# Weight sections of a two-layer encoder, fetched in one transfer or in two

## The chip, the cores and the metric

The kernel runs on one core of a Trainium2 chip. The metric is the device time of one execution in microseconds; lower is better. Before the change it is 2028.26 us, the median of three runs (2027.85 to 2029.19).

## What is computed

A two-layer encoder over 2048 tokens of width 1024. Each layer normalizes its input, projects it to eight parts of 512 columns, runs chunked softmax attention with a relative bias on one half of the heads and chunkwise retention on the other, gates both and projects back. Cut to what matters:

```python
def hybrid_layer(x, norm_gain, w_in, w_out, rel_bias, cos, sin):
    hn = rms_norm(x, norm_gain)
    proj = hn @ w_in                                   # (2048, 1024) @ (1024, 4096)
    aq, ak, av, ag, rq, rk, rv, rg = jnp.split(proj, cuts, axis=-1)
    ya = chunked_rel_attention(aq, ak, av, rel_bias)   # 8 heads x 64, own chunk and 8 before
    yr = chunkwise_retention(rq, rk, rv, cos, sin)     # 4 heads x 128
    y = jnp.concatenate([ya * silu(ag), yr * silu(rg)], axis=-1)
    return x + y @ w_out

def reference(x, positions, norm_gain, w_in, w_out, rel_bias, final_gain):
    for layer in range(2):
        x = hybrid_layer(x, ...)
    return rms_norm(x, final_gain)
```

All inputs are float32. w_in is (2, 1024, 4096), w_out is (2, 1024, 1024).

## The kernel before

Each float32 operand is split into a high and a low float16 part, and each product is taken as three float16 matmuls (high x high, high x low, low x high). A layer has four head groups (`s` = 0 to 3), each with two attention heads and one retention head, and each group goes over four blocks of 512 tokens (`n`). For a block, `dense_T` (L867) makes the transposed projections q, k and the two rotated parts, `dense_V` (L888) the projections with tokens on the partitions, and `attention` is interleaved with the dense matmuls of the next block: scores at L936 and L937, softmax on VectorE and ScalarE (L940 to L945), the low part of the probabilities `pq` on GpSimd (L946), a transpose of them by DMA into `pT` (L948), and the matmuls with v at L956 to L958. After the four groups the output projection `dO` (L1286) follows.

A group needs eight weight sections, each 1024 rows x 128 columns of w_in (512 KB): four for `dense_T` (tiles `stT`, by `prep_T`) and four for `dense_V` (`stV`, by `prep_V`). The output projection needs eight sections of w_out per layer (`stO`, by `prep_O`), and `prep_Omax` reads the same eight once more ahead of that for the scale (`stO0m`, `stO1m`). `load_sec` fetches one section into a tile of 128 partitions x 8 x 128 float32, where the row `k * 128 + p` lies on partition `p`, so each partition gets eight runs of 512 bytes. The tile is then squared and summed on ScalarE (L394), scaled and rounded to the high part on ScalarE (L419), and its low part is taken on VectorE (L422). The tiles come from a pool of three buffers (`w4`), shared with other staging tiles.

At the change of layers the sections for the next layer's first group are fetched by the other branch of `load_sec` (`halves`, L385), which has two smaller tiles and a transfer of 256 KB for each. The very first group of layer 0 is loaded with an order written by hand (`LOADS`): three of its sections by `load_sec` (names that begin with `T0_0`), the rest by transfers of their own.

All transfers are issued from SyncE, in one queue. On the compute engines the order is that of the program text, which tables such as `BESIDE` and `PLAN` set: a preparation is a generator, and each of its steps runs at a given half round of the dense matmuls. SyncE's order after the first block is left to the framework's scheduler. The program gives its transfers eight completion semaphores in turn. Among the transfers between which the loads stand are `swp` (halves of a rotated part swapped, L802 and L803), q and k copies (L771, L782 to L785), tables (`tabc`, `tabs`), outputs of a block (`y_d`, L971 and L1063) and the transposes of the normalized rows (`hTh`, `hTl`, L312 and L313).

Of the kernel before, what the change touches and what calls it, by code (L numbers as in the profile page):

```python
# [93 lines left out]
def hybrid_trunk(ctx: ExitStack, tc: tile.TileContext, x, pos, gain, gcol, w_in, w_out, rel, fgain,  # L94
# [4 lines left out]
    KT = D // P  # L99
# [4 lines left out]
    act, dve, pool, pe, sp = nc.scalar, nc.vector, nc.gpsimd, nc.tensor, nc.sync  # L104
# [269 lines left out]
    def load_sec(src, nm, halves=False):  # L374

        v = src.rearrange("(k p) c -> p k c", p=P)
        if not halves:
            st = w4.tile([P, KT, P], F32, tag="w4", name=f"st{nm}")
            sp.dma_start(st, v)
            return [(st, 0, KT)]  # L380
        h = KT // 2
        st = [b2.tile([P, 3 - i, 512], F16, tag=("rot2", "rot3")[i], name=f"st{nm}_{i}") for i in range(2)]
        st = [t_[:, 0:2].rearrange("p a c -> p (a c)").bitcast(F32).rearrange("p (k c) -> p k c", c=P) for t_ in st]
        for i in range(2):
            sp.dma_start(st[i], v[:, i * h:(i + 1) * h, :])  # L385
        return [(st[i], i * h, (i + 1) * h) for i in range(2)]
# [53 lines left out]
    class Sections:  # L440
# [12 lines left out]
        def load(self, j):  # L453
            o = TSEC[j] * 512 + self.s * P
            self.sts.append(load_sec(w_in[self.l, :, o:o + P], f"{self.nm}{j}", self.halves))
# [47 lines left out]
    def prep_V(l, s, g):  # L503
# [6 lines left out]
        def ld(j):  # L510
            o = VSEC[j] * 512 + c0
            sts.append(load_sec(w_in[l, :, o:o + P], f"{nm}{j}"))
# [39 lines left out]
    def prep_V_next(l, g):  # L552

        nm = f"V{l}_0"
        src = [w_in[l, :, VSEC[j] * 512:VSEC[j] * 512 + P] for j in range(4)]
        sts = [load_sec(src[j], f"{nm}{j}", True) for j in range(2)]
        yield
        for j in (2, 3):
            st = b2.tile([P, KT, P], F32, tag="q", name=f"st{nm}{j}")
            sp.dma_start(st, src[j].rearrange("(k p) c -> p k c", p=P))  # L560
            sts.append([(st, 0, KT)])
        yield
        g.vh = b3.tile([P, KT, 512], F16, tag="wh", name=f"wh{nm}")
        g.vl = b3.tile([P, KT, 512], F16, tag="wl", name=f"wl{nm}")
        hi, lo = ([w_[:, :, j * P:(j + 1) * P] for j in range(4)] for w_ in (g.vh, g.vl))
        m = [lowp_of(sumsq(sts[j], f"{nm}{j}", hi[j]), f"{nm}{j}") for j in range(2)]
        yield
        m2, m3 = (sumsq(sts[j], f"{nm}{j}", hi[j]) for j in (2, 3))
        m.append(lowp_of(m2 + m3, f"{nm}2"))
        yield  # L570
        yield
        iv = [None] * 3
        for j in (2, 0, 1):
            sv, iv[j] = norm_scale(allsum(m[j], f"{nm}{j}"), f"{nm}{j}", gains[l].i)
            for i in ((2, 3) if j == 2 else (j,)):
                yield from convert(sts[i], hi[i], lo[i], sv)
        yield from V_units(l, 0, g, iv, nm)
        g.vdone = 4
# [963 lines left out]
    for t in range(8, 16):  # L1542
        rows = late[t - 8] if t < 12 else xs0[t % 2]
        v = rows.bitcast(F16)
# [5 lines left out]
    for l in range(DEPTH):  # L1550
        gO = [Grp(), Grp()]
        go = Grp()
        for s in range(NSW):
            g = grp(l, s)
            for n in range(NS):
                first = (l, s, n) == (0, 0, 0)
                if not first:
                    st = states.setdefault((l, s, n), St())
                    dT = dense_T(l, s, n, g, st)
                else:  # L1560
                    st = st0
# [129 lines left out]
```

## Time and profile before

| what | value |
|---|---|
| median of three runs | 2028.26 us |
| profiled execution, its own time | 2024.23 us |
| its span (first to last instruction) | 2022.5 us |
| TensorE busy | 1986.4 us, 98% |
| VectorE, ScalarE, GpSimd busy | 1298.3, 1156.4, 464.0 us |
| granted TensorE clock, mean | 0.998 |
| bytes moved by DMA | 315.23 MB, mean 156 GB/s |
| transfers of the dynamic queue | 67.5% of the time of 16 DMA engines |

Times in the profile are microseconds from the span's start unless marked ns. PE is TensorE's matmul, PEld its weight load, DVE VectorE, ACT ScalarE, POOL GpSimd, SP SyncE; a q behind an engine's name means its sequencer, so SPq rows are issues of transfers, with the time that an issue kept the queue. A row of the timeline has start, duration, engine, line, operation, tiles and, in brackets, the idle time before it with what ended it. A row of the waits has the waiting engine and line, what it waited for, total us, number of times and the longest. A row of windows has the stretch, its length, then for TensorE, its weight loads, VectorE, ScalarE and GpSimd the busy time and the number of instructions, then the granted clock, the DMA engines' busy share and GB/s. A row of a line's instructions has minimum, median and maximum ns; "DMA to landing" is the time from issue to completion.

### The profile page before, as it was taken

The page shows a single profiled execution, that of the slowest core. Times are in us where ns is not written, and L with a number is a line of the kernel's source. Part 1 is how long each engine was busy: PE and PEld are TensorE (multiplying, and loading weights), DVE is VectorE, ACT ScalarE, POOL GpSimd, SP SyncE. Part 2 cuts the span into 40 slices and gives each one's busy share as a digit, 9 for nine tenths or more (in the row PEclk, how much of TensorE's full clock was granted, in tenths as well). Part 3 has the DMA queues.
Part 4 walks back from the last instruction along what each step waited for, and adds up shares of the span by engine and source line. Part 5 has one row for each costly group of instructions (what it writes and reads, how often), then busy time and mean ns, then how long its engine had stood idle before and what let it go on. Part 6 is the DMA issues. An engine that isn't in the chain of part 4 may idle for free.

```text
span 2022.5 us, 39569 instructions
## 1 busy us (share of the span) xinstructions
PE 1986.4 (98%) x14006; PEld 1047.4 (52%) x14006; DVE 1298.3 (64%) x4014; ACT 1156.4 (57%) x2525; POOL 464.0 (23%) x521
## 2 busy tenths in 40 slices
PE   6999999999999999999999999999999999999998
PEld 5444555555555555554444555555555555555444
DVE  7777867566656665766645557665666676557543
ACT  7666766466666655655445556655665665456432
POOL 1442222222222222220001222222222222222100
PEclk9999999999999999999999999999999999999999
DMA  9698765465586655899973547554755766558874
GB/s 265 137 185 189 156 147 132 103 140 129 131 182 139 155 128 104 191 243 269 241 180 95 123 99 161 122 119 100 158 123 133 168 162 160 120 119 191 207 205 125
DMA packets 654104, 315.23 MB, mean 156 GB/s; under 512 B 467505, under 2 KB 610865, under 8 KB 653905
## 3 DMA queue, kind: packets, MB, share of 16 engines
q1 hardware_dynamic: 653904, 312.70, 67.5%
q8 instruction: 110, 1.80, 0.4%
q14 instruction: 90, 0.73, 0.1%
HBM read 123.26 MB, written 41.98 MB: 82 GB/s over the span
## 4 chain that ended last, share of the span: by engine, by line
PE 88%; DVE 4%; DMA 3%; ACT 2%; SPq 1%; issue 1%; POOL 0%; ACTq 0%; POOLq 0%; DVEq 0%
PE dT L867 31%; PE dV L888 29%; PE dO L1286 13%; PE r L996 4%; PE S L937 3%; PE S L936 3%; PE o L956 2%; PE o L957 2%; PE o L958 2%; DMA pT<-pq 1%; PE dT L848 1%; DVE sc L940 1%; DMA swp<-raw 1%; ACT sc L943 0%; SPq L948 0%
## 5 line engine op out<-in xcount | busy, mean ns | idle before, releaser
L946 POOL TENSOR_TENSOR pq<-sc,pq 128x640 f16<-128x640 f32 (+4 forms) x256 | 328.7, 1284 | 1169.2 <-issue 717.0
L943 ACT ACTIVATE sc<-sc,mq,cT 128x640 f32<-128x640 f32 (+4 forms) x256 | 218.4, 853 | 426.3 <-DVE mq L942 423.6
L888 PE MATMUL dV<-whV,hTh 128*128 128x512 f16 x1024 | 352.3, 380 | 0.9 <-DVE gt L906 0.9
L888 PE MATMUL dV<-wlV,hTh 128*128 128x512 f16 x1024 | 352.3, 380 | 0.0
L888 PE MATMUL dV<-whV,hTl 128*128 128x512 f16 x1024 | 352.0, 379 | 0.0
L867 PE MATMUL dT<-hTh,whT 128*128 128x512 f16 x1008 | 346.6, 379 | 0.8 <-DMA hTh<-hTl 0.8
L867 PE MATMUL dT<-hTl,whT 128*128 128x512 f16 x1008 | 346.6, 379 | 0.0
L867 PE MATMUL dT<-hTh,wlT 128*128 128x512 f16 x1008 | 346.6, 379 | 0.0
L940 DVE CUSTOM_DVE_ANT_0 sc<-S,bias 128x640 f32<-128x640 f32 (+4 forms) x256 | 188.6, 737 | 192.8 <-PE S L937 191.6
L888 PEld LDWEIGHTS <-hTh 128*128 128x128 f16 x2048 | 196.6, 98 | 209.8 <-DVE gt L906 1.9
L867 PEld LDWEIGHTS <-whT 128*128 128x128 f16 x2016 | 192.3, 98 | 199.1 <-DVE gt L906 1.3
L945 ACT ACTIVATE pq<-sc 128x640 f16<-128x640 f32 (+4 forms) x256 | 171.5, 670 | 8.1
L1286 PE MATMUL dO<-whO,yly 128*128 128x512 f16 (+2 forms) x456 | 170.7, 375 | 1.6 <-DMA yly<-rly 1.6
L1286 PE MATMUL dO<-whO,yhy 128*128 128x512 f16 (+2 forms) x456 | 170.8, 375 | 0.3 <-DMA yhy<-rhy 0.3
L1286 PE MATMUL dO<-wlO,yhy 128*128 128x512 f16 (+2 forms) x456 | 170.8, 375 | 0.0
L888 PEld LDWEIGHTS <-hTl 128*128 128x128 f16 x1024 | 99.4, 98 | 104.3 <-issue 0.8
L867 PEld LDWEIGHTS <-wlT 128*128 128x128 f16 x1008 | 97.2, 98 | 100.7
L936 PE MATMUL S<-k,q 128*128 128x128 f16 (+3 forms) x592 | 142.4, 267 | 0.4 <-DVE mq L940 0.4
L1286 PEld LDWEIGHTS <-yhy 128*128 128x128 f16 x912 | 88.4, 98 | 101.6 <-DMA yhy<-rhy 0.8
L956 PE MATMUL o<-v,pT 128*128 128x65 f16 x1120 | 129.4, 193 | 9.7 <-DVE rl L962 4.6
L937 PE MATMUL S<-k,q 128*128 128x128 f16 (+3 forms) x592 | 129.7, 267 | 0.0
L957 PE MATMUL o<-v,pT 128*128 128x64 f16 x1120 | 129.7, 195 | 0.0
(374 smaller groups left out, 3388.8 us busy)
## 6 DMA issues: line engine op xcount, KB each, us to landing
q<-qq SPq DMA_DIRECT2D x128, 128.0 KB, 2.4
yyy<-y_d SPq DMA_DIRECT2D x32, 512.0 KB, 4.7
stT<-in_w_in_dram SPq DMA_DIRECT2D x27, 512.0 KB, 4.9
stV<-in_w_in_dram SPq DMA_DIRECT2D x26, 512.0 KB, 4.5
k<-kk SPq DMA_DIRECT2D x128, 64.0 KB, 2.1
tabc<-tab SPq DMA_DIRECT2D x32, 256.0 KB, 2.8
tabs<-tab SPq DMA_DIRECT2D x32, 256.0 KB, 2.7
y_d<-yr SPq DMA_DIRECT2D x128, 64.0 KB, 2.0
```

Of the source, the lines that this page charges most:

```text
L867: pe.matmul(ps, w_[:, j, kt, :], h_[:, kt, :], start=(m == 0), stop=(m == 23))
L888: pe.matmul(ps, h_[:, kt, a * P:(a + 1) * P], w_[:, kt, :], start=(m == 0), stop=(m == 23))
L936: pe.matmul(o, st.q[:, hx, 0, cs], k_, start=True, stop=False)
L937: pe.matmul(o, st.q[:, hx, 1, cs], k_, start=False, stop=True)
L940: dve.tensor_tensor_reduce(out=v, in0=S[:, 0:w], in1=g.bias[hx][:, 640 - w:640], scale=1.0, scalar=-3.0e38, op0=ALU.add, op1=ALU.max, accu ...
L943: act.activation(v, v, AF.Exp, bias=m[:, 0:1], scale=g.c[:, 0:1])
L945: act.activation(pq[:, 0:w], v, AF.Copy)
L946: pool.tensor_tensor(pq[:, w:2 * w], v, pq[:, 0:w], op=ALU.subtract)
L956: pe.matmul(o[:, 0:65], u.p[:, b, :], v_[:, 0:65], start=(b == 0), stop=False)
L957: pe.matmul(o[:, 0:64], u.p[:, b, :], v_[:, 65:129], start=False, stop=False)
L996: pe.matmul(out_, w_, m_, start=(i == 0), stop=(i + 1 == len(pairs)))
L1286: pe.matmul(ps, h_[:, kt, :], w_[:, kt, c0:c1], start=(m == 0), stop=(m == 23))
```

## The change

A section whose name begins with `T0_0` is fetched as before. For every other section that `load_sec` fetches into one tile, the transfer is cut into two: the first four of the eight runs of every partition, and then the last four.

```diff
         v = src.rearrange("(k p) c -> p k c", p=P)
         if not halves:
             st = w4.tile([P, KT, P], F32, tag="w4", name=f"st{nm}")
-            sp.dma_start(st, v)
+            n_ = 1 if nm.startswith("T0_0") else 2
+            for i in range(n_):
+                ks = slice(i * KT // n_, (i + 1) * KT // n_)
+                sp.dma_start(st[:, ks, :], v[:, ks, :])
             return [(st, 0, KT)]
```

80 sections are cut (24 of `stT`, 24 of `stV`, 16 of `stO` and 16 of `stO0m` and `stO1m`), so SyncE has 1479 transfers in place of 1399. The rows of the four compute engines stand as before. All lines below the change move down by three: the load is L382 then, the transpose of pT L951.

SyncE's queue at the first section that is cut, in layer 0, where group 1's first section `stT_10` is fetched during group 0. Before:

```order
L312 DMA_TRANSPOSE hTh_3_152<-xa 128x8x128
L379 DMA stT_10_2389<-in_w_in_dram 128x8x128
L802 DMA swp_0_2_3_2086<-raw_0_2_2014 64x512
L803 DMA swp_0_2_3_2086<-raw_0_2_2014 64x512
L313 DMA_TRANSPOSE hTl_3_153<-xa 128x8x128
L948 DMA_TRANSPOSE pT_0_1_2_0_2082<-pq_0_1_2_0_2079 128x10x128
```

The same place after:

```order
L312 DMA_TRANSPOSE hTh_3_152<-xa 128x8x128
L382 DMA stT_10_2389<-in_w_in_dram 128x4x128 x2
L805 DMA swp_0_2_3_2086<-raw_0_2_2014 64x512
L806 DMA swp_0_2_3_2086<-raw_0_2_2014 64x512
L313 DMA_TRANSPOSE hTl_3_153<-xa 128x8x128
L951 DMA_TRANSPOSE pT_0_1_2_0_2082<-pq_0_1_2_0_2079 128x10x128
```

One row has become two in the same place; what stands behind is the same.

A little later, `stT_13`, the fourth section of that group, between a pT and the four copies of k. Before:

```order
L379 DMA stT_13_2732<-in_w_in_dram 128x8x128
L948 DMA_TRANSPOSE pT_0_2_0_1_2576<-pq_0_2_0_1_2573 128x10x128
L782 DMA k_0_3_2608<-kk_0_3_2609 64x512
L783 DMA k_0_3_2608<-kk_0_3_2609 64x512
L784 DMA k_0_3_2608<-kk_0_3_2609 64x512
L785 DMA k_0_3_2608<-kk_0_3_2609 64x512
L948 DMA_TRANSPOSE pT_0_2_1_0_2680<-pq_0_2_1_0_2677 128x10x128
```

After:

```order
L382 DMA stT_13_2735<-in_w_in_dram 128x4x128
L951 DMA_TRANSPOSE pT_0_2_0_1_2578<-pq_0_2_0_1_2575 128x10x128
L785 DMA k_0_3_2611<-kk_0_3_2612 64x512
L786 DMA k_0_3_2611<-kk_0_3_2612 64x512
L787 DMA k_0_3_2611<-kk_0_3_2612 64x512
L788 DMA k_0_3_2611<-kk_0_3_2612 64x512
L382 DMA stT_13_2735<-in_w_in_dram 128x4x128
L951 DMA_TRANSPOSE pT_0_2_1_0_2683<-pq_0_2_1_0_2680 128x10x128
```

Here the scheduler puts a transpose and four copies between the two halves. This is so at 12 of the 80 sections, at some of them with only a `y_d` between.

The scan of w_out in layer 0, group 2, where three sections of `stO0m` are issued in a row. Before:

```order
L948 DMA_TRANSPOSE pT_2_1_2_0_8061<-pq_2_1_2_0_8058 128x10x128
L379 DMA stO0m_8117<-in_w_out_dram 128x8x128
L379 DMA stO0m_8186<-in_w_out_dram 128x8x128
L379 DMA stO0m_8225<-in_w_out_dram 128x8x128
L1063 DMA y_d_110<-yr_2_5_8163 128x128
```

After:

```order
L951 DMA_TRANSPOSE pT_2_1_2_0_8083<-pq_2_1_2_0_8080 128x10x128
L382 DMA stO0m_8141<-in_w_out_dram 128x4x128 x2
L382 DMA stO0m_8211<-in_w_out_dram 128x4x128 x2
L382 DMA stO0m_8251<-in_w_out_dram 128x4x128 x2
L1066 DMA y_d_110<-yr_2_5_8188 128x128
```

Six issues stand where there were three.

## The prediction

> **What bounds the kernel now.** I read the page first (engine shares, the chain that ended last), then the windows by stage, then the waits of TensorE and of SyncE's transfer queue, then the issue rows of the weight loads, and last the timeline around the loads that have something urgent behind them.
>
> ```profile
> PE 1986.4 (98%) x14006; PEld 1047.4 (52%) x14006; DVE 1298.3 (64%) x4014; ACT 1156.4 (57%) x2525; POOL 464.0 (23%) x521
> PE 88%; DVE 4%; DMA 3%; ACT 2%; SPq 1%; issue 1%; POOL 0%; ACTq 0%; POOLq 0%; DVEq 0%
> ...
> 200.00:850.00 650.00, 649.96 (x4867) 349.24 (x4866) 425.83 (x1407) 391.03 (x893) 160.07 (x178) 1.00 0.63 139
> 1000.00:1850.00 850.00, 849.91 (x6112) 449.32 (x6110) 529.49 (x1700) 485.82 (x1109) 190.65 (x217) 1.00 0.61 137
> ```
>
> TensorE is busy for 1986.4 of 2022.5 us. In the two long windows (first numbers after the length: TensorE) it is idle 0.04 us of 650 and 0.09 us of 850, at a granted clock of 1.00. Most of the changed loads lie there, and nothing that makes a load faster can be worth anything there. A change can cost, if it makes something late that TensorE takes just in time. What that would be is in the waits:
>
> ```profile
> PEld L956 <- DMA pT<-pq: 14.1, 13, 5.1
> PE o L956 <- DMA pT<-pq: 3.7, 3, 1.8
> ...
> SPq L948 <- POOL rss L1057: 218.2, 74, 5.8
> SPq L948 <- POOL pq L946: 194.7, 129, 10.6
> ...
> SPq L379 <- DMA x_d<-xxy: 4.6, 1, 4.6
> ```
>
> TensorE waits for the transposed probabilities pT. They leave by the transpose at L948, on the same queue as the weight loads of L379. The queue itself mostly waits in front of L948 for GpSimd, in 129 + 74 = 203 of 256 cases: there it is ahead of its work, and a longer issue somewhat earlier is swallowed. Only loads that run without a pause into an L948 count.
>
> **The change part by part.** The bytes, the pieces of 512 bytes (128 columns of 4) and all engine instructions stay; 80 loads become 160 transfers. What each half costs the queue is read from the loads of 512 KB (L379) and from the layer change, which already fetches halves (L385):
>
> ```profile
> L379 SPq DMA_DIRECT2D stT<-in_w_in_dram x27: 378/539/1675, 4.5 to 1497.4; - x27
> L379 SPq DMA_DIRECT2D stO1m<-in_w_out_dram x8: 383/552/1737, 1505.9 to 1572.1; - x8
> DMA to landing us min/median/max: 3.9/4.9/8.5
> ...
> L385 SPq DMA_DIRECT2D stT<-in_w_in_dram x8: 379/428/1219, 838.7 to 953.6; - x8
> DMA to landing us min/median/max: 3.1/4.2/5.3
> ```
>
> A whole load takes 0.539 us to issue, a half 0.428, with some 0.07 us to the next: 2 x 0.428 + 0.07 - 0.539 = 0.39, so I take 0.4 us more per load. [...] Over 80 loads that is 32 us of queue time; it counts at these places alone.
>
> First place: the first changed load, layer 0, second group.
>
> ```profile
> 157.51 0.57 SPq L379 DMA_DIRECT2D stT<-in_w_in_dram  x1
> 158.18 0.59 SPq L802 DMA_DIRECT2D swp<-raw  x1
> 158.82 0.59 SPq L803 DMA_DIRECT2D swp<-raw  x1
> 159.50 1.48 SPq L313 DMA_TRANSPOSE hTl<-xa  x1
> 161.08 4.75 SPq L948 DMA_TRANSPOSE pT<-pq  x1
> ...
> 162.92 0.38 PE L888 MATMUL dV<-whV,hTl 128*128 128x512 f16 x1
> 167.88 0.23 PE L956 MATMUL o<-v,pT 128*128 128x65 f16 x1 [4.58 <-DVE rl L962]
> ...
> 163.00:168.00 5.00, 0.42 (x5) 0.12 (x4) 2.26 (x8) 2.13 (x4) 0.57 (x1) 0.82 0.64 113
> 168.00:173.00 5.00, 5.00 (x29) 2.62 (x29) 4.96 (x13) 2.56 (x8) 1.83 (x1) 0.50 1.08 292
> ```
>
> The queue runs from 157.51 to 165.83 without a pause, and TensorE stands for 4.58 us behind it (and then runs at clock 0.50 for 5 us). Here 0.4 us more in front goes straight to TensorE: +0.4.
>
> Second place: two loads in front of a pT.
>
> ```profile
> 260.06 1.31 SPq L379 DMA_DIRECT2D stT<-in_w_in_dram  x2
> 261.60 1.53 SPq L1063 DMA_DIRECT2D y_d<-yr  x1
> 263.17 0.43 SPq L971 DMA_DIRECT2D y_d<-ya  x1
> 264.65 1.33 SPq L948 DMA_TRANSPOSE pT<-pq  x1
> ```
>
> The queue pauses from 263.60 to 264.65, 1.05 us; 2 x 0.4 = 0.8 is swallowed: 0.
>
> Third place: three loads of the scan for w_out's maximum.
>
> ```profile
> 575.29 2.94 SPq L379 DMA_DIRECT2D stO0m<-in_w_out_dram  x3
> 578.84 1.16 SPq L1063 DMA_DIRECT2D y_d<-yr  x1
> ...
> 581.05 0.38 SPq L714 DMA_DIRECT2D tabs<-tab  x1
> 581.89 1.58 SPq L948 DMA_TRANSPOSE pT<-pq  x1
> ```
>
> The pauses are 578.23 to 578.84 and 581.43 to 581.89, 0.61 + 0.46 = 1.07 us; 3 x 0.4 = 1.2, so 0.13 us is left. I count it whole, as if TensorE had no reserve. The same group in layer 1 I count as covered.
>
> Fourth place: a load of w_out directly ahead of a pT.
>
> ```profile
> 1807.22 0.57 SPq L379 DMA_DIRECT2D stO<-in_w_out_dram  x1
> 1807.91 3.47 SPq L948 DMA_TRANSPOSE pT<-pq  x1
> ...
> 1812.01 1.89 PE L888 MATMUL dV<-whV,hTh 128*128 128x512 f16 x8
> 1813.93 0.20 PE L956 MATMUL o<-v,pT 128*128 128x65 f16 x1
> ```
>
> TensorE ended its eight matmuls at 1813.90 and took pT at 1813.93, so there is no reserve: +0.4.
>
> Sum: 0.4 + 0 + 0.13 + 0.4 = 0.93 us. The profiled execution took 2024.23 us (span 2022.5), which would become 2025.2; the median of the three timed runs is 4.0 us above it, and the forecast goes from that: 2028.26 + 0.93 = **2029.2 us**.
>
> Two smaller edits. In 12 of the 80 pairs the scheduler puts other transfers between the halves (at stT_13 a pT and the four k copies), so these go out behind half a load, not a whole one. TensorE is idle 0.04 us of 650 there, so the gain is at most that: 0. And the program hands out eight completion semaphores in turn, so a transfer waits for the eighth before it to land, and a load now takes two of the eight. The longest such wait in the rows above is 4.6 us, once, on a store; with landings of 4.2 us and eight issues of 0.4 us or more ahead I count 0, up to a microsecond where loads stand together.
>
> [...]
>
> **The rivals.** *Slower, the queue has no room after all.* Three whole loads took 2.94 us, 0.98 each, where they stand together, and single issues reach 1.7. Let a half add p instead of 0.4. The places then cost p at the first and the fourth, 2p - 1.05 at the second, 3p - 1.07 at the third: 7p - 2.12 in all. From p = 0.88 this passes 4.06 us; at p = 1.2 (my estimate between 0.98 and 1.7) it is 6.3 us, **2034.6**; at 1.7 it is 9.8, 2038. For it: the issue rows just named. Against: the median of L385.
>
> *Slower, the weights land late.* If halves do not overlap, a load lands 2 x 4.2 - 4.9 = 3.5 us later.
>
> ```profile
> DMA to landing us min/median/max: 4.8/5.9/6.3
> ...
> 580.24 1.04 ACT L394 ACTIVATE stO0m<-stO0m 128x1024 f32<-128x1024 f32 x1
> ```
>
> The row is that of the three loads issued from 575.29: the first landed at 580.09 and ScalarE read it at 580.24. 3.5 us more would hold ScalarE for 3.35 us, and the probabilities behind it; once in each layer that is up to 6.7 us, **2035.0**. Against: all three landed within 6.3 us of issue, so loads do overlap, and elsewhere they come well ahead of use.
>
> *Faster, the standstill at 163 us gives way.* If with shorter transfers the swp copies and pT come 4.6 us sooner, TensorE keeps its clock too, and half of the 5 us at clock 0.50 is won: 4.6 + 2.5 = 7.1 us, **2021.2**.
>
> ```profile
> 895.00:905.00 10.00, 8.17 (x73) 4.36 (x72) 8.21 (x22) 6.43 (x12) 3.56 (x5) 1.00 1.04 243
> ```
>
> For it: an idle stretch of 1.8 us there left the clock at 1.00, so a shorter standstill would not bring it down. [...] Against: both halves of that load still stand directly in front of the copies.
>
> That the change does not do what it says is out but for the 12 pairs.
>
> **How the numbers follow.** The bound of 0.2%, about what a measurement of this kernel can tell from no change, is 4.06 us. Little change: 0.45. Slower by the queue: 0.30; by late weights: 0.08. Faster by the standstill: 0.17. So faster 0.17, same 0.45, slower 0.38. The likeliest case alone reaches from 2026 (the first and fourth places swallow it, and a microsecond of luck) to 2032. The whole range, 2022 to 2037, takes in the slower cases up to p = 1.55 and the lesser half of the faster one.
>
> **What would show it.** The new line (L382) should show 3 whole loads and 160 halves, these near 0.43 us each; SyncE's waits for GpSimd and VectorE should shrink by some 30 us in all; TensorE's two long windows should stay within 1 us of full. The forecast is wrong if the pT waits grow past 20 us, if ScalarE waits for stO0m or stT, or if the standstill at 163 us is gone.

## The result, and the profile after

The changed kernel takes 2025.0 us, median of 13 runs (2020.6 to 2028.45), beside 2028.39 us for the kernel before (13 runs, 2025.87 to 2033.01). The ratio is 0.998, 95% interval 0.9972 to 0.9988: **faster by about 4 us** (3.4 us between the medians), where the forecast said 2029.2 us, 0.93 us slower than before. The time lies within the stated range of 2022 to 2037, but "faster" had a chance of 0.17. The profiled execution after took 2026.06 us (span 2024.3), that of before 2024.23: the one pair of traces goes the other way from the medians. Single executions of one kernel scatter by 1.7 us (standard deviation of the 147 runs of the kernel before that were timed beside the experiments), so one trace against one cannot show 4 us. What follows therefore reads places, and the same place in many traces.

Three fences answer to those of before. The page's line of busy times, and its chain:

```profile
PE 1987.4 (98%) x14006; PEld 1047.4 (52%) x14006; DVE 1298.6 (64%) x4014; ACT 1157.4 (57%) x2525; POOL 464.6 (23%) x521
PE 89%; DMA 4%; DVE 4%; issue 1%; ACT 1%; SPq 1%; POOL 0%; POOLq 0%; ACTq 0%; DVEq 0%
```

The two long windows:

```profile
200.00:850.00 650.00, 649.25 (x4877) 349.22 (x4876) 425.68 (x1401) 390.44 (x892) 160.62 (x177) 1.00 0.63 139
1000.00:1850.00 850.00, 849.80 (x6111) 449.55 (x6109) 529.38 (x1699) 486.23 (x1109) 190.45 (x217) 1.00 0.60 137
```

TensorE's waits for pT (total us, times, longest):

```profile
PEld L959 <- DMA pT<-pq: 15.6, 14, 3.0
...
PE o L959 <- DMA pT<-pq: 6.6, 8, 1.9
```

In the two long windows TensorE is idle 0.75 and 0.20 us. The 0.75 us is one stop for a pT, right behind the forecast's second place:

```profile
266.72 0.20 PE L959 MATMUL o<-v,pT 128*128 128x65 f16 x1 [0.75 <-DMA pT<-pq]
```

In the trace of before the same matmul lost 0.04 us. That was a good execution: in the 13 other traces that have the two loads of that place whole, it lost 0 to 1.81 us, 0.69 on average. So the first window had a little to win or to lose before the change too, and one trace does not say which it was. TensorE's waits for pT in all are no shorter in this one execution. What did change are the loads themselves. Rows of L382 (issue in ns, minimum, median and maximum, then landing of all its transfers):

```profile
L382 SPq DMA_DIRECT2D stV<-in_w_in_dram x48: 383/499/1526, 202.6 to 1626.8; - x48
L382 SPq DMA_DIRECT2D stO1m<-in_w_out_dram x16: 384/499/1280, 1507.8 to 1575.5; - x16
...
DMA to landing us min/median/max: 2.9/3.5/8.6
```

Transfers by size (median us from issue to landing):

```profile
stV<-in_w_in_dram SPq DMA_DIRECT2D x52, 256.0 KB, 3.4
stO<-in_w_out_dram SPq DMA_DIRECT2D x32, 256.0 KB, 3.5
```

The same two rows of before:

```profile
stV<-in_w_in_dram SPq DMA_DIRECT2D x26, 512.0 KB, 4.5
stO<-in_w_out_dram SPq DMA_DIRECT2D x16, 512.0 KB, 5.2
```

A half lands 3.4 to 3.5 us after its issue, where a whole section took 4.5 and 5.2. The second half is issued some 0.57 us after the first. Of the 68 pairs that stand together the first half lands 3.2 us and the second 3.6 us after its own issue, and both are there 4.3 us after the first issue (medians), so a section in two is there *sooner* than in one.

The place of the forecast's first and largest term, SyncE's queue and then TensorE in the timeline of after:

```profile
156.53 1.15 SPq L382 DMA_DIRECT2D stT<-in_w_in_dram  x2
157.79 0.49 SPq L805 DMA_DIRECT2D swp<-raw  x1
158.32 0.59 SPq L806 DMA_DIRECT2D swp<-raw  x1
159.02 1.40 SPq L313 DMA_TRANSPOSE hTl<-xa  x1
160.53 2.38 SPq L951 DMA_TRANSPOSE pT<-pq  x1
162.96 1.13 SPq L382 DMA_DIRECT2D stT<-in_w_in_dram  x2
...
164.91 0.20 PE L959 MATMUL o<-v,pT 128*128 128x65 f16 x1 [2.49 <-DVE rl L965]
```

The two windows of after at that place:

```profile
163.00:168.00 5.00, 3.09 (x26) 1.76 (x27) 4.89 (x16) 3.71 (x10) 1.56 (x1) 0.77 1.11 254
168.00:173.00 5.00, 5.00 (x28) 2.22 (x27) 4.89 (x15) 2.74 (x7) 0.27 (x1) 0.89 1.10 224
```

The load keeps the queue 1.15 us instead of 0.57, and pT is issued 4.00 us after it instead of 3.57. But pT's own issue takes 2.38 us in place of 4.75, TensorE waits 2.49 us in place of 4.58, and the clock (last column but two of the windows) is at 0.77 and 0.89 where it was 0.82 and 0.50. By the clock records it is at 0.50 for 3.41 us here (from 165.66 us) and was for 6.83 us (from 166.25): the one window and the two windows at clock 0.50 of which the expectations below speak. These are two single executions; averages over many traces stand further down.

### The profile page after: what moved, and what is told of

It reads as the page before. It is cut to its first block, busy times and chain, and to the rows that moved or that the text cites. A ratio compares the mean times of both kernels' runs of the same rounds, so it can differ in the third digit from the quotient of the medians.

```text
span 2024.3 us, 39702 instructions
## 1 busy us (share of the span) xinstructions
PE 1987.4 (98%) x14006; PEld 1047.4 (52%) x14006; DVE 1298.6 (64%) x4014; ACT 1157.4 (57%) x2525; POOL 464.6 (23%) x521
## 4 chain that ended last, share of the span: by engine, by line
PE 89%; DMA 4%; DVE 4%; issue 1%; ACT 1%; SPq 1%; POOL 0%; POOLq 0%; ACTq 0%; DVEq 0%
PE dT L870 31%; PE dV L891 30%; PE dO L1289 13%; PE r L999 4%; PE S L940 3%; PE S L939 3%; DMA pT<-pq 2%; PE o L959 2%; PE o L960 2%; PE o L961 2%; PE dT L851 1%; DVE sc L943 0%; DMA x_d<-hTl 0%; DMA yly<-rly 0%; DMA xa<-in_x_dram 0%
```

## The experiments

All kernels below differ from the kernel before in the one place that the change touches, unless said otherwise; the code line that says how many pieces a section gets is shown. Each was timed beside the kernel before on its chip. The matmuls and the other engines' instructions stand in the same order in all of them. SyncE's other transfers do too, with three exceptions, in which the scheduler also moved some of them: `e1_seven_one` at two places, `e3_four` at seven, and `e3_columns` at some twenty.

### One section, all but one, and an unequal cut

```diff
-            sp.dma_start(st, v)
+            n_ = 1                                                    # e1_null
+            n_ = 2 if nm == "T0_10" else 1                            # e1_first_only
+            n_ = 1 if nm.startswith("T0_0") or nm == "T0_10" else 2   # e1_not_first
+            for i in range(n_):
+                ks = slice(i * KT // n_, (i + 1) * KT // n_)
+                sp.dma_start(st[:, ks, :], v[:, ks, :])
```

```diff
-            sp.dma_start(st, v)
+            cut = (0, KT) if nm.startswith("T0_0") else (0, KT - 1, KT)   # e1_seven_one
+            for a, z in zip(cut, cut[1:]):
+                sp.dma_start(st[:, a:z, :], v[:, a:z, :])
```

> The kernel before with the loop written but one transfer for every section, so every instruction stands as before. All theories: 1.000 of the time before, within 0.1%. It is there for the spread and for a second trace of the old order. Place theory (the gain comes at the first cut load, 157 us): TensorE again stands for 4 to 5 us at 163 us and the clock then shows 0.50 for two windows, about 6.8 us. Accident theory (the long standstill in the first trace came from where a fetch of instructions fell): the standstill at 163 us is well under 4 us here, or over 5.5.

Measured 0.9994 (0.9985 to 1.0003). Its trace, with every instruction as before, stands 3.44 us at 163 us and keeps the full clock there (1.00 from 163 to 173 us): standstill and clock at one place differ from run to run.

> Only the first of the 80 sections (stT_10, layer 0, group 1, issued at 157.5 us) is cut into two; the other 79 stay whole. Place theory (all of the gain is that the load ahead of the swp copies and pT gives way sooner, 2 us of standstill and 1.7 us of half clock): 0.998 of the time before, -3.5 to -4 us, with the standstill at 163 us near 2.7 us and one window at clock 0.50. Sum theory (79 other loads each give a little where TensorE waits, at 0 to 190 and 850 to 930 us): -0.2 us or less, 1.000. Forecast's price (+0.4 us of issue ahead of the copies): +0.4 us, 1.000.

Measured 0.9998 (0.9989 to 1.0007). The place looks as in the changed kernel (pT's issue, and TensorE's wait):

```profile
160.91 2.07 SPq L951 DMA_TRANSPOSE pT<-pq  x1
...
165.02 0.23 PE L959 MATMUL o<-v,pT 128*128 128x65 f16 x1 [2.24 <-DVE rl L965]
```

So the place does get shorter, but that is not the 4 us: by the interval it is 2.2 us at the most.

> 79 sections cut, stT_10 at 157.5 us left whole. Place theory: 1.000 of the time before (0 to +0.5 us), the standstill at 163 us as before, 4 to 5 us. Sum theory: 0.998, as with all 80 cut. Forecast's price: +0.5 us (the places at 575 and 1807 us).

Measured 0.9986 (0.9978 to 0.9995): most of the gain without the first section. That all of it comes from that place has fallen.

> All 80 sections cut as in the change, but into seven and one of the eight runs of a partition (448 and 64 KB), so that the number of transfers, the turn of the completion semaphores and the issue time in the queue are those of the change, while the first transfer is nearly as long as a whole one. Length theory (a transfer of half the size starts to move its bytes sooner, what stands behind it follows sooner): little of the gain, 0.9995 or more, the standstill at 163 us 4 us or more. Turn theory (what helps is that two transfers take two of the eight semaphores, so that waits fall on other transfers): all of the gain, 0.998. Forecast's price: +0.9 us, 1.0005.

Measured 0.9982 (0.9974 to 0.9991): all of the gain with a very uneven cut. The length theory as written fell: the first piece need not be short. It is also what the turn theory forecast, and no run below rules that theory out. So cut, a section lands only 0.18 us sooner than whole (57 sections whose pieces stand together, place by place against the two traces of the uncut order), so its own landing is hardly what the gain hangs on. What waits behind it is quicker all the same: at the first place pT's issue takes 2.86 us, at the fourth 1.95.

### By parts of the program

```diff
+            n_ = 2 if nm[:4] in ("T0_1", "V0_1") else 1     # e2_group1, 8 sections
+            n_ = 2 if nm.startswith("O0_") else 1           # e2_out0, 8
+            n_ = 2 if nm.startswith("O1_") else 1           # e2_out1, 8
+            n_ = 1 if nm[:4] in ("T0_0", "T0_1", "V0_1") or nm[:3] in ("O0_", "O1_") else 2   # e2_middle, 56
```

> Only the 8 sections of layer 0's group 1 are cut (issued between 157 and 210 us, the one stretch after the start in which TensorE waits and sections are fetched). Early theory (what is gained is gained here: the standstills at 163, 173 and 188 us shrink, and with them the half clock that follows): 0.998 to 0.9985 of the time before, -3 to -4 us. Spread theory (a little from every group of cut loads near a wait): 0.9995, -1 us. Nothing here (as when the first of them alone was cut, 0.9998): 1.000.

Measured 0.9985 (0.9976 to 0.9994).

> Only the 8 sections of w_out of layer 0 are cut (issued between 650 and 842 us, ahead of the change of layers, where TensorE waits at 854 to 929 us for pT and for yly). Layer-change theory (the standstills between 850 and 930 us shrink): 0.9985, -3 us. Spread theory: 0.9995. Early theory: 1.000.

Measured 0.9983 (0.9974 to 0.9992).

> Only the 8 sections of w_out of layer 1 are cut (issued between 1700 and 1837 us; one wait of TensorE follows, at 1846 us, 0.2 to 1.2 us in the traces so far). All theories: 1.000, at the most -0.5 us. The forecast's price says +0.4 us (the place at 1807 us). A clear gain here would mean that the traces don't show where the time goes.

Measured 0.9995 (0.9986 to 1.0004). The trace at the place of the forecast's fourth term:

```profile
1807.42 1.17 SPq L382 DMA_DIRECT2D stO<-in_w_out_dram  x2
1808.70 2.08 SPq L951 DMA_TRANSPOSE pT<-pq  x1
```

> The other 56 sections are cut: groups 2 and 3 of layer 0, groups 1 to 3 of layer 1, and both scans of w_out. All of them are issued while TensorE is busy without a gap. Early and layer-change theory: 1.000. Spread theory: 1.000 too, since nothing waits there. If this one carries the gain (0.998 to 0.9985), the gain isn't where the cut loads are, and something that goes through the whole program (the turn of the eight completion semaphores, shifted by 56 transfers) carries it to the change of layers.

Measured 0.9999 (0.999 to 1.0008): the 56 sections fetched in the long windows are worth nothing that can be told from 1.000, within some 2 us either way. Their queue time, 56 x 0.4 = 22 us, cost the kernel 1.6 us at the most by the interval. TensorE is not full beside all of them, though: at 268 us it stands 2.24 us in this trace, for the pT behind the second place.

### More pieces, other pieces

```diff
+                cs = slice(i * P // n_, (i + 1) * P // n_)          # e3_columns
+                sp.dma_start(st[:, :, cs], v[:, :, cs])
+            n_ = 1 if nm.startswith("T0_0") else 4                  # e3_four
+            n_ = 2 if nm[:4] in ("T0_1", "V0_1") or nm.startswith("O0_") else 1   # e3_group1_out0
```

`e3_rows` leaves the sections whole and cuts `sp.dma_start(u.y, y_d[t])` and the load of `u.x` into two halves of 512 columns.

> All 80 sections in two transfers, as in the change, but cut by columns (64 and 64 of the 128), so each half has all eight runs of every partition, 256 bytes long: 2048 pieces for a section in place of 1024. The count of transfers, the turn of the completion semaphores and the issue time in the queue are those of the change. Landing theory (the change gains because a section cut in two has landed 0.48 us sooner, counted from its first issue, in 68 sections compared place by place, and what stands behind it 0.4 us sooner though issued 0.6 us later): with twice the pieces the section lands later than a whole one, by 0.5 us or more, and the gain is gone, 1.000 to 1.002. Turn theory (two transfers where there was one, whatever their landing): the gain stays, 0.998. Forecast's price: +0.9 us, 1.0005.

Measured 1.0042 (1.0029 to 1.0055, five runs): the same number of transfers, and 8.5 us slower than before. A section cut by columns lands no sooner than a whole one (0.01 us later on average, 56 sections compared in the same way), and this much the run shows of the pieces. ScalarE now waits for the scan of w_out; the rows of its waits:

```profile
ACT stO0m L397 <- DMA stO0m<-in_w_out_dram: 4.4, 3, 2.8
ACT stO1m L397 <- DMA stO1m<-in_w_out_dram: 4.3, 3, 2.9
```

And TensorE's first long window has a hole of 3.86 us, the second one of 1.96:

```profile
200.00:850.00 650.00, 646.14 (x4838) 346.65 (x4837) 421.16 (x1394) 385.89 (x887) 159.08 (x177) 1.00 0.67 138
1000.00:1850.00 850.00, 848.04 (x6086) 447.97 (x6085) 525.93 (x1686) 483.65 (x1102) 188.99 (x215) 1.00 0.63 136
```

This looks like the forecast's rival of the late weights, at the place it named. But the scheduler also moved other transfers here, above all transposes of pT, forward in SyncE's queue. In the changed kernel the six halves of the scan's three sections are issued in one row (572.84, shown further down). Here the queue reads:

```profile
574.26 2.69 SPq L382 DMA_DIRECT2D stO0m<-in_w_out_dram  x3
577.75 0.42 SPq L1066 DMA_DIRECT2D y_d<-yr  x1
578.22 0.43 SPq L382 DMA_DIRECT2D stO0m<-in_w_out_dram  x1
580.81 1.32 SPq L951 DMA_TRANSPOSE pT<-pq  x1
582.23 0.53 SPq L974 DMA_DIRECT2D y_d<-ya  x1
582.81 2.05 SPq L382 DMA_DIRECT2D stO0m<-in_w_out_dram  x3
```

The third of the three sections goes out 8.55 us after the first, beside 3.2 in the changed kernel, since a pT stands ahead of it for which the queue first stands idle for 2.16 us. ScalarE waits for it, and for a half behind the next pT, for 4.0 of the 4.4 us: these weights are late because they were asked for late, and from their issue they land in 3.3 to 4.5 us. TensorE's stops in the two windows all stand 6 to 15 us behind such a moved transpose; one of the two longest is this:

```profile
595.35 0.19 PE L959 MATMUL o<-v,pT 128*128 128x65 f16 x1 [1.75 <-DVE yr L1064]
```

So this run has two changes in one, the pieces and the order, and can't say what the pieces alone cost, or whether the turn theory holds. At the fourth place, where the order is that of the change, pT's issue is short here too (2.04 us); at the first place (1.43 us) pT stands one transfer further forward.

> All 80 sections in four transfers of 128 KB (two of the eight runs of a partition each). Landing theory: a section lands at the earliest when its fourth issue, some 1.7 us after the first, has taken its 2.5 to 3 us, so 4.4 us or more from the first issue, as with two; what is behind is issued 1.7 us later instead of 0.6: no more gain than with two, and part of it given back, 0.9985 to 1.0005. Turn theory: more gain than with two, 0.997. Forecast's price: 1.7 us of issue at each of the four places, 7 to 9 us slower, 1.004.

Measured 1.0014 (1.0005 to 1.0023): slower. Here the queue's price shows, first in TensorE's waits for pT:

```profile
PEld L959 <- DMA pT<-pq: 24.3, 19, 3.0
...
PE o L959 <- DMA pT<-pq: 13.5, 13, 2.3
```

Its two long windows are no longer full:

```profile
200.00:850.00 650.00, 647.42 (x4851) 347.28 (x4850) 421.60 (x1397) 387.91 (x889) 159.85 (x177) 1.00 0.63 138
1000.00:1850.00 850.00, 848.46 (x6089) 448.07 (x6088) 525.84 (x1690) 484.55 (x1106) 189.47 (x215) 1.00 0.59 136
```

A section in four ends its issue 1.64 us later than a whole one and lands 0.38 us sooner; with two it was 0.57 and 0.51. At the first and fourth places TensorE stands 2.67 and 0.00 us (counted as in the table further down), about as with halves, but the windows lose 2.58 and 1.54 us, with halves 0.75 and 0.20, all of it in waits for pT. That the queue has reserve for one more issue per section and not for three is the likely reading; the order of some other transfers also differs here, two transposes of pT among them.

> The 16 sections of the two parts that gained alone (group 1 of layer 0, 0.9985, and w_out of layer 0, 0.9983), the other 64 whole. If the gains add: 0.997, -6 us. If they share one stock (the change with all 80 cut has 0.998): 0.998, -4 us, and the other 64 sections are then worth nothing, for or against.

Measured 0.9981 (0.9972 to 0.999), median 2023.48 us: sixteen sections gain what all eighty gain.

> No section is cut; in place of that the 512-KB loads of whole rows around the change of layers and at the end (the 32 yyy and 32 loads of x rows, 128 pieces of 4096 bytes each) are cut in two by columns, 128 pieces of 2048 bytes each. Landing theory, if it holds for any transfer of 512 KB: each lands sooner (4.7 us now) and the waits at 888 to 927 us shrink, 0.9985. If it holds only for transfers of many small pieces: the second issue (0.5 us) stands in front of pT, yhy and yly in a queue without pauses, +0.5 to +3 us, 1.000 to 1.0015.

Measured 1.0004 (0.9996 to 1.0013). The loads of 4096-byte rows landed hardly sooner when cut: of the yyy pairs issued together the last half landed 4.59 us after the first issue, beside 4.67 for a whole one. These loads were also cut across their pieces, not between them. A clearly sooner landing was thus seen only at loads of 1024 pieces of 512 bytes that are cut between pieces.

### Near a wait of TensorE, and far from one

```diff
+            n_ = 2 if nm.startswith("T0_1") else 1                  # e4_T1
+            n_ = 2 if nm.startswith("V0_1") else 1                  # e4_V1
+            n_ = 2 if nm in ("O0_12", "O0_13") else 1               # e4_out0_last
+            n_ = 2 if nm.startswith("O0_") and nm not in ("O0_12", "O0_13") else 1   # e4_out0_first
```

`e5_near` cuts the sections of `e4_T1` and `e4_out0_last`, `e5_far` those of the other two.

> Of group 1 in layer 0 only the four stT sections are cut (issued between 157 and 195 us, among the standstills of TensorE at 163, 173 and 188 us). Place theory (a cut section helps only where TensorE waits within some microseconds for a transfer that stands behind it): all of group 1's gain, 0.9985. Shift theory (fewer transfers late somewhere changes how all that follows falls, wherever the cut is): half of it, 0.9992. Chance theory (the gains of 3 us in the two parts were scatter of the runs): 1.000.

Measured 0.9994 (0.9986 to 1.0003).

> Of group 1 only the four stV sections are cut (issued between 204 and 238 us, where TensorE is busy without a gap until 850 us). Place theory: 1.000. Shift theory: 0.9992. Chance theory: 1.000.

Measured 1.0007 (0.9998 to 1.0016).

> Of w_out's sections in layer 0 only the last two are cut (issued at 832 and 843 us, 12 us or more ahead of the first standstill at the change of layers). Place theory: all of the gain that the eight had, 0.9983. Shift theory: a quarter of it, 0.9996. Chance theory: 1.000.

Measured 1.0006 (0.9998 to 1.0015).

> Of w_out's sections in layer 0 the first six are cut (issued between 652 and 817 us, where TensorE is busy without a gap). Place theory: 1.000. Shift theory: three quarters of the gain that the eight had, 0.9987. Chance theory: 1.000.

Measured 0.9997 (0.9988 to 1.0005).

> Six of the sixteen sections that gained together (0.9981): the four stT of layer 0's group 1 and the last two of w_out in layer 0, those issued within 30 us of a wait of TensorE. Place theory: 0.998 to 0.9985, all of the gain of the sixteen. Shift theory (each cut section counts alike, wherever it stands): six sixteenths, 0.9993. If this run and the next both come out at 1.000, the sixteen together do what neither part does, and neither theory holds.

Measured 0.9993 (0.9985 to 1.0002).

> The other ten of the sixteen: the four stV of layer 0's group 1 and the first six of w_out in layer 0, issued while TensorE has no gap and 30 us or more from its next wait. Place theory: 1.000. Shift theory: ten sixteenths, 0.9988.

Measured 0.9995 (0.9986 to 1.0004). No part of the sixteen stands apart from 1.000 by itself. Place and shift theory can't be told apart by these six: each effect is 1 to 2 us, and an interval is 1.8 us to either side.

## Where the time came from

**What is shown place by place.** 17 traces have the sections whole or in equal halves. Between TensorE's 2000th and 5000th matmul (301 to 702 us) 14 of them take 401.4 to 401.5 us (the others 401.7, 401.8 and 402.4), and from the 7000th to the 12000th (1010 to 1707 us) 16 take 696.9 (the other 697.2). Nearly all scatter, and with it the gain, lies outside: at the start, from 144 to 301 us, at the change of layers, and behind 1707 us. Two places can be averaged, since a trace has the load there either whole or cut (TensorE's stop is the one ahead of its next matmul with a pT, from start to start less the 0.22 us that a matmul takes back to back, which is 0.16 us more than the brackets of the rows show):

| place | load | traces | pT's issue, us | load to pT landed, us | TensorE stands, us |
|---|---|---|---|---|---|
| first, 157 us | whole | 11 | 3.73 (3.10 to 4.75) | 9.28 | 3.47 (2.89 to 4.75) |
| first, 157 us | cut | 6 | 2.56 (2.07 to 3.31) | 8.50 | 2.77 (2.40 to 3.69) |
| fourth, 1807 us | whole | 14 | 3.21 (2.70 to 3.48) | 6.52 | 0.21 (0 to 0.64) |
| fourth, 1807 us | cut | 3 | 1.64 (1.40 to 2.08) | 5.62 | 0.00 |

The forecast put +0.4 us on each. Measured are -0.7 and -0.2, on average: at the first place the ranges overlap. Three more places have a pT directly behind a section. Its issue takes 3.00 us behind a whole section and 2.13 behind a cut one at 255 us (13 and 3 traces), 3.21 and 1.97 at 817 us (10 and 6), but 1.24 and 1.20 at 1500 us (7 and 3), so the long issue is frequent behind a whole section and not the rule. And over 68 sections whose halves stand together (16 traces, each section's mean when cut less its mean when whole), a section has landed 0.49 us sooner (standard error 0.05) although its issue ends 0.58 us later; the next transfer, where it follows without a pause (29 sections), lands 0.54 us sooner (0.16) although it is issued 0.53 us later.

**What is shown in sum.** Fitting the 16 ratios (the change, the null kernel, and all those with halves or seven and one) by a sum of parts, each ratio uncertain by 0.00045, gives by least squares, with 95% bounds of 1.2 to 1.4 us on each: group 1's stT -2.1 us, its stV +0.5, w_out of layer 0 -1.9 (first six) and +0.1 (last two), the 56 in the middle +0.2, w_out of layer 1 -0.6; sum -3.8, to 1.0 us either way (the residuals' squares add to 14.6 for 10 degrees of freedom, so a sum of parts is not contradicted). This is an estimate, and a fit by hand-chosen parts. Its bounds are too narrow: the kernels of one batch share a chip and the runs of the kernel before, and the four `e2` runs all lie below the fit (by 0.4 to 1.8 of their uncertainty), the four `e4` runs all above (by 1.0 to 1.4). The four parts of the sixteen sections come to 1.0004 together in `e4` and to 0.9988 in `e5`, where the sixteen in one kernel had 0.9981. Whether the gain differs from chip to chip was not tried.

**The clock's share.** Each run lists its mean granted clock: 0.99754 over 147 runs of the kernel before, 0.99815 over 68 runs of the six kernels that were clearly faster (the change, e1_not_first, e1_seven_one, e2_group1, e2_out0, e3_group1_out0). The difference times 2024 us is 1.2 us, with a standard error of 0.3, out of the 3.2 us by which the means of these runs differ (2028.06 and 2024.90): by this estimate some two fifths of the gain are matmuls that ran at full clock, and the rest is time in which TensorE stood. The share is more likely too high than too low, since the six kernels were chosen by their times, and a run with a slower clock is a longer one (of the 147, the 16 runs at 0.996 take 2029.3 us on average, the 21 at 0.999 take 2027.6). The mean also counts a slow stretch at the end, which in every trace begins 2.6 us or more after the last matmul (before 3.8 us, after 4.8) and costs nothing.

**What stays open.** That group 1's stT sections gain fits the place theory: they stand among the standstills from 163 to 188 us. It also shows in the traces, though the split was made after the fact: TensorE's 2000th matmul starts at 298.8 us in the five traces with all four of them in halves (298.4 to 299.4) and at 300.3 us in the ten with all four whole (299.1 to 302.4), 1.4 us sooner with a standard error of 0.4. That the first six of w_out gain, fetched some 37 us and more ahead of the next wait, does not fit, and the traces show no place for it: from the 5000th to the 7000th matmul the four traces with all eight sections of layer 0's w_out in halves take 310.1 us on average and the nine with all of them whole 310.5, a difference of half its standard error. Intervals of 0.9997 and of 0.9983 (all eight) leave room for less. Why a transpose gets through sooner behind two transfers than behind one, and a section of 1024 pieces lands sooner in halves, was not tried: no run took these apart. The turn theory is not settled either. Halves and seven-and-one both take two of the eight semaphores and both gain, and in the third kernel with two transfers for a section, the one cut by columns, the order differs. That a transfer waits for the eighth before it to land is seen in the trace of before three times (1.5, 1.3 and 0.2 us, all in the first 47 us) and in that of after four times (1.1 us at the longest, in the same stretch); the 4.6 us that the prediction counts to these waits is a wait for a store two transfers earlier.

## Why the prediction was wrong

**The bound, and the windows that nothing can gain in:** near. The 56 sections there came out at 0.9999. But the first window was read as full from one execution, and in others TensorE stands up to 1.81 us in it, behind the second place.

**The price of an issue:** near. The forecast said 0.43 us for a half and 0.39 more for a section; the medians are 0.50 to 0.53, and a section's issue ends 0.58 us later. At the third place the six issues take this, against 2.94 us for three before:

```profile
572.84 4.21 SPq L382 DMA_DIRECT2D stO0m<-in_w_out_dram  x6
...
579.39 2.07 SPq L951 DMA_TRANSPOSE pT<-pq  x1
```

Issues can be longer behind loads (a pT's 3.47 us beside 1.33 after a pause, both in the prediction's rows); no run shows what makes them longer. The six issues are 1.27 us more, 0.42 for a section. pT goes out 6.55 us after the first load, beside 6.60 before: the pauses swallowed all of it, so the term is 0 in place of 0.13. The second place's term of 0 is not confirmed: TensorE stopped there for 0.75 us, which lies within what executions with whole loads show. SyncE's waits for GpSimd and VectorE fell from 900.0 to 869.8 us (sums over the view's rows), by 30.2 where some 30 were forecast; the kernel before, run again as e1_null, has 911.8, so part of the agreement is luck.

**The step that failed** is the first place: "Here 0.4 us more in front goes straight to TensorE: +0.4", and the fourth by the same reasoning; the two are 0.8 of the sum's 0.93 us. It took the issue of pT as a fixed length that is moved back. It is not: at these places the transpose's issue is held for 2.7 us and more behind one load of 512 KB; behind a cut load it starts later and on average ends sooner, in halves, in four, or in seven and one. In place of +0.4 and +0.4 stand -0.7 and -0.2 us. The fourth place after the change shows it best, beside 0.57 and 3.47 us before:

```profile
1808.98 1.17 SPq L382 DMA_DIRECT2D stO<-in_w_out_dram  x2
1810.26 1.40 SPq L951 DMA_TRANSPOSE pT<-pq  x1
```

From the load's issue to the end of pT's issue it was 4.16 us, and is 2.68. The row with 4.75 us for a single pT issue stood in the prediction's own fence and was read as queue time in front, not as something that the load ahead may set; it was also the longest of 11 such issues, 3.73 us on average. The two places make up 0.9 of the 3.4 to 4 us. For the rest the step that failed is that the sum had no term by which a cut load could gain at all; group 1's part shows at the start (1.4 us, the first place included), and the cause of what is left stays open.

**The rival "slower by the queue":** its mechanism is likely real, but not at this size: e3_four lost 4.1 us in the long windows in waits for pT. **"Late weights":** refuted for the halves of the change, which overlap: two halves issued 0.6 us apart are both there after 4.3 us (median), where one alone takes 3.4 to 3.5 us (ScalarE's waits after the change hold no stO0m). In e3_columns ScalarE does wait for them, but there they are issued later.

**The rival "faster, the standstill at 163 us gives way":** right in its direction, and its counter-argument ("both halves of that load still stand directly in front of the copies") did not decide, since the pT gets through sooner behind two halves that stand in the same place as the whole load. Its size was too large: the standstill shrinks by 0.7 us on average and doesn't go away, and by e1_first_only the place is 2.2 of the 4 us at the most.

**What the forecast had no term for, too,** is the change of layers. The profiled execution of before (2024.23 us, where 147 runs of that kernel lie from 2023.69 to 2031.7) had its best passage there: 307.9 us from TensorE's 5000th to its 7000th matmul, beside 308.8 to 314.0 in the 16 other traces. It looked like a place with little to win. The gain of 0.9983 with layer 0's w_out alone points there, but the traces do not show it.

## What to carry to other kernels

Price a transfer ahead of an urgent one by when the urgent one lands, not by when it is issued: the issue of a transpose behind a long load of many small pieces is no constant (at the first place 3.10 to 4.75 us behind a whole load, 2.07 to 3.31 behind a cut one). Cutting such a load in two is worth trying where something urgent stands behind it; four transfers were too many here (1.0014). Where a scheduler orders the queue, compare its order before and after every edit: an experiment on the pieces can turn out to be one on the order. A window that is full in one execution need not be full in the next (0 to 1.81 us lost at one matmul, in 14 traces). An effect of 0.2% is read from a dozen runs and from the same place in many traces, since one trace against one can have the wrong sign.

## What the runs showed of the hardware

A transfer costs packets beside its pieces. The queue's row in the page of before (packets, MB, share of 16 engines):

```profile
q1 hardware_dynamic: 653904, 312.70, 67.5%
```

Of after:

```profile
q1 hardware_dynamic: 655184, 312.70, 67.5%
```

Of e3_columns:

```profile
q1 hardware_dynamic: 737104, 312.70, 70.1%
```

80 more transfers are 1280 more packets, 16 for each; the columns add 81,920 more, one for every piece that became two, and 2.6 points of the engines' time for the same bytes.

The clock does not follow the length of a standstill alone. In e1_null a wait of 3.44 us at 163 us was followed by full clock, in the changed kernel one of 2.49 us by 3.41 us at 0.50 (windows of e1_null, to be read beside those of after):

```profile
163.00:168.00 5.00, 1.56 (x25) 1.09 (x24) 3.37 (x11) 3.25 (x6) 0.49 (x1) 1.00 0.71 170
168.00:173.00 5.00, 5.00 (x24) 2.06 (x22) 4.96 (x14) 2.36 (x10) 1.84 (x1) 1.00 1.14 278
```

The slow stretches ahead of the last matmul last 3.41 or 6.83 us in every trace that has one (by the traces' clock records: before 6.83 us, after twice 3.41). What decides whether a standstill is followed by one was not shown.
